# Transposing the memory's keys by crossbar DMA in a fused transformer block

## The chip, the cores and the metric

The kernel runs on one core of one Trainium2 chip. A core has TensorE (matrix products, into PSUM), VectorE, ScalarE and GpSimd (element-wise work), SyncE (here it only issues DMAs), 16 DMA engines, an on-chip memory of 128 partitions (SBUF) and eight PSUM banks of 128 x 512 f32. Each engine works through its own instructions in the order in which the program gives them, and waits on semaphores where it needs another engine's result. The metric is the device time of one execution in microseconds (us). In the profile PE is TensorE, PEld its weight load, DVE is VectorE, ACT ScalarE, POOL GpSimd, SP SyncE.

## What is computed

One layer on 256 tokens of width 1024, all in f32: a mixer (pooling over windows for half of the width, causal attention with 8 heads for the other half), cross attention to a memory of 256 rows with 4 heads of 256, and a convolutional feed-forward part. The change concerns the keys of the cross attention:

```python
def _cross_attention(h, m, w_xq, w_xkv, xq_norm_g, xk_norm_g, w_xo):
    q = (h @ w_xq).reshape(B, S, XATTN_HEADS, XATTN_HEAD_DIM)
    kv = (m @ w_xkv).reshape(B, M, 2, XATTN_HEADS, XATTN_HEAD_DIM)
    k, v = kv[:, :, 0], kv[:, :, 1]
    q = _rms_norm(q, xq_norm_g)
    k = _rms_norm(k, xk_norm_g)
    s = jnp.einsum('bshd,bmhd->bhsm', q, k) * (XATTN_HEAD_DIM ** -0.5)
    p = jax.nn.softmax(s, axis=-1)
    o = jnp.einsum('bhsm,bmhd->bshd', p, v).reshape(B, S, D_MODEL)
    return o @ w_xo
```

## The kernel before

**Products in two halves.** Each f32 operand is written as a high part (rounded to the type of TensorE's fast f32 products) and the low rest. `part_h` makes the high part on ScalarE (L269 without, L271 with a scale), `part_l` the rest on VectorE (L275, L277). Activations lie as 128 x 2048 tiles of such pairs (`cat`, `h`, `kx`, `xq` and so on; four buffers, called `pair`). The weights come from HBM in chunks of 1 MB into a ring of three (`raw`), loaded on SP's queue (L182). A chunk is two units; each unit is cast by ScalarE (`split_h`, L210, into `wh`) and its rest formed by VectorE (`split_l`, L221, into `wl`). `need(u)` issues these ahead of the unit u that TensorE uses, by up to five units, fewer at some stages. A load waits until the chunk three before it has been split.

**Stages.** TensorE runs: products of x for keys, queries, values and the pooled half; the memory's keys in two products of four units each (`a_chunk(18, ...)` for heads 0 and 1, `a_chunk(22, ...)` for heads 2 and 3); the mixer's output w_out (`resid_stage`, from u = 26, eight blocks f of 2.8 us, result `h`); w_xq (from u = 34, eight blocks, result `xq`, through L892 on ScalarE, L893 on VectorE, then `part_h`, a square and `part_l`); the memory's values; cross attention's output; the feed-forward part.

**Order by hand.** Whatever accompanies the products is written as generators ("jobs"). After every few matmuls the program calls `tick()`, and each job then issues its next piece; `wait(n)` lets n ticks go by. The constants WAIT_... are these numbers of ticks. A tick is two of the eight parts of a block in the stages w_out and w_xq, that is a quarter of a block. Within a tick the jobs take their turn in the order in which they were started: attention before the pool, the pool before the scores' later parts and before the key jobs. An engine's order is the order in which pieces were issued, so a piece that waits holds up all later ones of its engine. `finish` calls ticks until jobs have ended; between the memory's keys and w_out four ticks pass so, while the attention's last pieces are issued.

**The key job.** `key_job(c, bks)` takes the two PSUM banks of heads 2c and 2c+1 (each 128 memory rows x 512, two heads of 256). Five ticks after its start ScalarE sums the squares (L727), then `head_scale` makes 1/sqrt by Newton steps on GpSimd (`rs4y`, `rs5y`, L249 to L252). Eight ticks later VectorE scales the first bank into the SBUF tile `kn` (L735), seven ticks later the second. Nine ticks later TensorE transposes the first head in four 128 x 128 transposes (L743) into one bank, and ScalarE's `part_h` writes `kx`; thirteen ticks later `part_l`, two ticks later the second head in the same manner. The job ends 57 ticks after its start. `x_job(hp)` uses `kx` in the score products of w_xq's stage (in `three`, L286 to L288): the first, for heads 0 and 1, is issued eight ticks after w_xq's fourth block and once both key jobs have ended.

**The pool and the attention at the start of w_out.** The pool's result is evacuated in two steps of two groups (`evac_split` in `pool_job`: L271 and L277 per group, two groups to a bank), two ticks apart. Then the attention's four banks are evacuated (`evac_split` in `attn_job`, L269 and L275). All go into `cat`, w_out's input.

**Buffers.** PSUM banks are handed out by `bank()` from eight; small SBUF tiles of 128 x 512 f32 by `t2()` from nineteen.

## Time and profile before

| | |
|---|---|
| time of the kernel, median of 3 runs (least to most) | 380.37 us (379.93 to 380.6) |
| span of the profiled execution, first to last instruction | 378.1 us |
| median of the runs above that span | 2.27 us |
| instructions | 5948 |
| mean granted TensorE clock | 0.999 |
| moved from and to HBM | 67.71 MB read, 1.05 MB written |

The span is the profiled execution's own time as the profile gives it; what an execution takes before its first and after its last instruction is in the runs' times alone. The page gives the busy time of each engine, then the chain of work that ended last, then groups of instructions. A line of the timeline has the start (us from the span's start), the duration, the engine, the line of the kernel, the operation, the tiles written and read, and in brackets the engine's idle time before it with the instruction that ended it. Consecutive instructions of one kind are merged (x2, x4), so their duration is that of the whole run. Durations of pipelined instructions overlap: what one costs its engine is the distance from its start to the next one's.

### The profile page before, as it was taken

Reading aid. Unit: us, or ns where it says so; the run is one execution under the profiler, and the core shown is the slowest. Engines: PE = TensorE matmul, PEld = TensorE weight load, DVE = VectorE, ACT = ScalarE, POOL = GpSimd, SP = SyncE. Lnnn points to the kernel's source line nnn. Section 1 sums busy time; section 2 is a strip of 40 time slices with the busy share of each in tenths; the row PEclk is TensorE's granted clock in tenths of the full one; section 3 lists DMA queues with packets and bytes.
Section 4 is the critical chain, followed back from the end, with each engine's and each line's share of the span. In section 5 each row is a group of like instructions: output and inputs, shape, how many; then the busy total and the mean of one; then the engine's idle time right before and its main releaser. Section 6 shows DMA issues by size and latency. Waiting matters only on the chain.

```text
span 378.1 us, 5948 instructions
## 1 busy us (share of the span) xinstructions
PE 373.9 (99%) x2154; PEld 325.7 (86%) x2154; DVE 317.6 (84%) x572; ACT 248.2 (66%) x483; POOL 70.6 (19%) x151
## 2 busy tenths in 40 slices
PE   9999999999999999999999999999999999999996
PEld 7888888888888988898888888888888888888885
DVE  4699999979878969689979999999999999654461
ACT  5767986977567665855665588778877786633210
POOL 0253886043731142101220000000000000000000
PEclk9999999999999999999999999999999999999999
DMA  8995372454505636263635155665555645364500
GB/s 265 421 383 217 121 327 93 146 208 139 198 5 217 224 111 225 109 224 112 219 118 221 59 179 210 223 220 184 179 206 213 224 136 199 128 246 161 201 16 28
DMA packets 12412, 69.13 MB, mean 183 GB/s; under 512 B 1376, under 2 KB 2784, under 8 KB 4832
## 3 DMA queue, kind: packets, MB, share of 16 engines
q1 hardware_dynamic: 12096, 68.24, 50.1%
q10 hardware_dynamic: 288, 0.52, 0.4%
q8 instruction: 17, 0.28, 0.3%
q14 instruction: 11, 0.09, 0.1%
HBM read 67.71 MB, written 1.05 MB: 182 GB/s over the span
## 4 chain that ended last, share of the span: by engine, by line
PE 99%; DVE 0%; issue 0%
PE bank L301 42%; PE bank L300 22%; PE bank L414 8%; PE bank L419 8%; PE bank L416 8%; PE bank L1065 1%; PE bank L288 1%; PE bank L286 1%; PE bank L287 1%; PE bank L372 1%; PE bank L572 1%; PE bank L1067 1%; PE bank L611 1%; PE bank L883 0%; PE bank L743 0%; PE bank L494 0%
## 5 line engine op out<-in xcount | busy, mean ns | idle before, releaser
L221 DVE TENSOR_TENSOR wl<-raw,wh 128x1024 fp32r<-128x1024 f32 (+1 forms) x127 | 150.0, 1197 | 3.9 <-ACT wh L210 3.9
L210 ACT CAST wh<-raw 128x1024 fp32r<-128x1024 f32 (+1 forms) x125 | 126.0, 1028 | 35.1 <-DMA raw<-wpack 31.0
L301 PE MATMUL bank<-hs,wh 128*128 128x512 f32 x304 | 105.4, 391 | 0.0
L300 PE MATMUL bank<-hs,wl 128*128 128x256 f32 x304 | 85.2, 280 | 0.0
L301 PEld LDWEIGHTS bank<-hs,wh 128*128 128x128 f32 x304 | 56.9, 187 | 12.4
L300 PEld LDWEIGHTS bank<-hs,wl 128*128 128x128 f32 x304 | 57.5, 189 | 0.0
L301 PE MATMUL bank<-act,wh 128*128 128x512 f32 x154 | 53.4, 391 | 0.0
L300 PE MATMUL bank<-act,wl 128*128 128x256 f32 x154 | 43.2, 280 | 0.0
L998 ACT ACTIVATE y<-up,sc 128x256 f32<-128x256 f32 x44 | 26.2, 603 | 22.3 <-DVE up L985 17.7
L301 PE MATMUL bank<-h,wh 128*128 128x512 f32 x112 | 39.4, 394 | 0.0
L1005 DVE SCALAR_TENSOR_TENSOR y<-up,sc,y 128x255 f32<-128x255 f32 (+1 forms) x88 | 36.6, 476 | 0.0
L301 PEld LDWEIGHTS bank<-act,wh 128*128 128x128 f32 x154 | 28.8, 187 | 6.3
L300 PE MATMUL bank<-h,wl 128*128 128x256 f32 x112 | 31.7, 283 | 0.0
L300 PEld LDWEIGHTS bank<-act,wl 128*128 128x128 f32 x154 | 29.1, 189 | 0.0
L301 PEld LDWEIGHTS bank<-h,wh 128*128 128x128 f32 x112 | 21.0, 188 | 4.6
L1069 DVE TENSOR_TENSOR o<-bank,sc 128x256 f32<-128x256 f32 x8 | 3.4, 424 | 24.5 <-PE bank L301 21.4
L301 PE MATMUL bank<-cat,wh 128*128 128x512 f32 x62 | 21.8, 393 | 0.0
L301 PE MATMUL bank<-ox,wh 128*128 128x512 f32 x62 | 21.6, 394 | 0.0
L271 ACT ACTIVATE h<-sc 128x256 fp32r<-128x256 f32 x16 | 8.2, 510 | 20.3 <-DVE sc L789 20.2
L300 PEld LDWEIGHTS bank<-h,wl 128*128 128x128 f32 x112 | 21.2, 189 | 0.0
L414 PE MATMUL bank<-wh,mg 128*128 128x512 f32 x64 | 20.7, 405 | 0.0
L797 POOL TENSOR_TENSOR h_acc<-h_sq,h_acc 128x256 f32<-128x256 f32 x14 | 12.9, 921 | 41.6 <-ACT h_sq L796 41.5
(253 smaller groups left out, 712.2 us busy)
## 6 DMA issues: line engine op xcount, KB each, us to landing
raw<-wpack SPq DMA_DIRECT2D x59, 1024.0 KB, 4.8
raw<-wpack SPq DMA_DIRECT2D x4, 512.0 KB, 7.3
mraw<-memT SPq DMA_DIRECT2D x4, 256.0 KB, 8.3
out<-o SPq DMA_DIRECT2D x8, 128.0 KB, 1.9
sc<-xpack SPq DMA_DIRECT2D x3, 256.0 KB, 5.1
raw<-wpack ACTq DMA_DIRECT2D x2, 256.0 KB, 3.5
raw<-wpack SPq DMA_DIRECT2D x2, 256.0 KB, 4.6
tab<-table SPq DMA_DIRECT2D x1, 480.0 KB, 8.8
```

The source lines that it names most:

```text
L210: copy(split[u][0][:, r], unit(u)[:, r])
L221: dve.tensor_tensor(l[:, r], unit(u)[:, r], h[:, r].bitcast(F32), op=ALU.subtract)
L271: act.activation(h, src, AF.Copy, scale=scale)
L286: pe.matmul(o, stat[0], mov[0], start=start, stop=False)
L300: pe.matmul(b[:, 0:n], stat[1], mov[:, 0:n], start=start, stop=False, skip_group_check=not wide_first)
L301: pe.matmul(b, stat[0], mov, start=False, stop=stop, skip_group_check=not wide_first)
L414: pe.matmul(bk[tt], a[tt][0], wv[0], start=k == 0, stop=False)
L416: pe.matmul(bk[tt], a[tt][1], wv[0], start=False, stop=False)
L419: pe.matmul(bk[tt], a[tt][0], wv[1], start=False, stop=k == KT - 1)
L797: pool.tensor_tensor(acc, sq, acc, op=ALU.add)
L998: act.activation(y[:, g * S:(g + 1) * S], src[:, g * S:(g + 1) * S], AF.Identity, bias=col(sc, C_CB + f), scale=col(sc, C_CW + 2 * 2 * NFF ...
L1005: dve.scalar_tensor_tensor(yy[:, j:], uu[:, :S - j], col(sc, C_CW + (2 - j) * 2 * NFF + f), yy[:, j:], op0=ALU.mult, op1=ALU.add)
```

## The change

The sixteen transposes on TensorE and the four banks for them go. In their place, for each of the two key jobs: ScalarE splits each scaled tile `kn` (128 x 512 f32) into two planes of 16-bit halves, lower halves first, then upper ones (128 x 1024 half-words, tile `kp`); SP issues a crossbar-transposing DMA from `kp` to `kf` for each of the two tiles; ScalarE then joins the halves, two copies of 512 half-words for each head, into a tile `kT` that has the layout of the old PSUM bank. `part_h` and `part_l` read `kT` in SBUF. Two key jobs make four splits, four transposing DMAs and eight joins.

The pauses of the job change too. The first tile's split follows its scaling with no tick between for heads 0 and 1, after one tick for heads 2 and 3; the second tile is scaled six ticks after the first tile's split and split three ticks (one tick) later; the DMAs follow three (two) ticks later, the first join twenty (eighteen) ticks after them. Six tiles for each job are taken from the nineteen `t2` buffers.

```diff
-WAIT_KEY = [0, 8, 7, 2, 0, 13, 5]
+WAIT_KEY = [0, 8, 6, 0, 0, 0, 5]
+WAIT_FLAT = [[0, 3, 3, 20, 1, 4], [1, 1, 2, 18, 2, 4]]
...
         yield from wait(WAIT_KEY[1])
+        flat = []
         for mt in range(TT):
             for i in range(2):
                 r = slice(i * XD, (i + 1) * XD)
                 dve.tensor_scalar(kn[c, mt][:, r], bks[mt][:, r], col(y, 2 * mt + i), None, op0=ALU.mult)
-            yield from wait(WAIT_KEY[2])
+            yield from wait(WAIT_FLAT[c][mt])
+            planes = t2(f"kp{c}{mt}").bitcast(U16)
+            act.copy(planes.rearrange("p (z n) -> p z n", z=2),
+                     kn[c, mt].bitcast(U16).rearrange("p (n z) -> p z n", z=2))
+            flat.append((planes, t2(f"kf{c}{mt}").bitcast(U16)))
+            if mt == 0:
+                yield from wait(WAIT_KEY[2])
+        pauses = WAIT_FLAT[c]
+        yield from wait(pauses[2])
+        for planes, to in flat:
+            nc.sync.dma_start_transpose(to.rearrange("p (g s) -> p g s", g=8), planes)
+        yield from wait(pauses[3])
         for i in range(2):
             h = 2 * c + i
-            yield from wait(WAIT_KEY[3])
-            b = bank()
-            for dd in range(2):
-                for mt in range(TT):
-                    pe.transpose(b[:, (dd * 2 + mt) * P:(dd * 2 + mt + 1) * P],
-                                 kn[c, mt][:, i * XD + dd * P:i * XD + (dd + 1) * P], ident)
-            bb = b.rearrange("p (d s) -> p d s", d=2)
-            yield from wait(WAIT_KEY[4])
+            kT = t2(f"kT{c}{i}")
+            for mt in range(TT):
+                act.copy(kT.bitcast(U16).rearrange("p (d m s z) -> p m z d s", d=2, m=2, z=2)[:, mt],
+                         flat[mt][1].rearrange("p (z i d s) -> p i z d s", z=2, i=2, d=2)[:, i])
+                yield from wait(pauses[4])
+            bb = kT.rearrange("p (d s) -> p d s", d=2)
             part_h(kxv[0][:, 2 * h:2 * h + 2], bb)
-            yield from wait(WAIT_KEY[5])
+            yield from wait(pauses[5])
             part_l(kxv[1][:, 2 * h:2 * h + 2], bb, kxv[0][:, 2 * h:2 * h + 2])
```

More of the change, by code (lines that the diff above doesn't have):

```diff
@@ L12 @@
 I32 = mybir.dt.int32
+U16 = mybir.dt.uint16
 AF = mybir.ActivationFunctionType
```

## The prediction

> **What bounds the kernel now.** I read the page first, then the chain that ended last, then the matmuls around the work that the change takes off TensorE.
>
> ```profile
> PE 373.9 (99%) x2154; PEld 325.7 (86%) x2154; DVE 317.6 (84%) x572; ACT 248.2 (66%) x483; POOL 70.6 (19%) x151
> PE 99%; DVE 0%; issue 0%
> ```
>
> TensorE is busy 99% of the span and makes up 99% of the chain, at full granted clock. So any time that its queue is spared comes off the end, and any gap that opens in it is added. The other engines matter only where TensorE comes to wait for them. Here is what one group of key transposes (L743) costs:
>
> ```profile
> 102.56 0.39 PE L301 MATMUL bank<-cat,wh 128*128 128x512 f32 x1
> 102.79 0.28 PE L300 MATMUL bank<-cat,wl 128*128 128x256 f32 x1
> 102.91 0.39 PE L301 MATMUL bank<-cat,wh 128*128 128x512 f32 x1
> 103.14 0.60 PE L743 MATMUL bank<-tab,kn 128*128 128x128 f32 x4
> 103.50 0.36 PE L300 MATMUL bank<-cat,wl 128*128 128x256 f32 x1
> 103.70 0.40 PE L301 MATMUL bank<-cat,wh 128*128 128x512 f32 x1
> ```
>
> Columns: start, duration, engine, line. Durations overlap, so starts have to be compared. From one L301 to the next is 0.35 us without transposes (102.56 to 102.91), and 0.79 with four between (102.91 to 103.70). A group costs 0.44 us, not the 4 x 0.27 that its instructions last.
>
> **What it removes.** Four such groups:
>
> ```profile
> L743 PE MATMUL bank<-tab,kn x16: 270/272/273, 92.3 to 115.5; 128*128 128x128 f32 x16
> ```
>
> Sixteen transposes are four groups of four; at the same price each, 4 x 0.44 = 1.76 us leave TensorE. The PSUM banks that go with them are not scarce: no matmul in this stretch starts late for one.
>
> **What it adds to ScalarE.** Four copies that split a 128x512 f32 tile into planes (1024 half-words per partition each) and eight that join 512 half-words. Nearest rows by element count:
>
> ```profile
> L210 ACT CAST wh<-raw 128x1024 fp32r<-128x1024 f32 x14 | 14.3, 1038 | 0.0
> L206 ACT CAST misc<-raw 128x512 fp32r<-128x512 f32 x3 | 1.8, 618 | 2.8 <-DMA raw<-wpack 2.8
> L269 ACT CAST kx<-bank 128x512 fp32r<-128x512 f32 x4 | 2.2, 574 | 0.0
> 111.43 1.98 ACT L210 CAST wh<-raw 128x1024 fp32r<-128x1024 f32 x2
> ```
>
> 4 x 1.04 + 8 x 0.62 = 9.1 us. No row shows 16-bit or strided elements; half of this (twice the elements in a given time) or double are the bounds, and I take the rows. The casts into kx stay, from SBUF at 0.62 instead of 0.57. What counts is where these copies stand in ScalarE's queue.
>
> **First place: the start of the w_out stage.** The first split of heads 0 and 1 follows the scaling of `kn` (L735) with no tick between. It therefore precedes, in ScalarE's queue, the pool's second evacuation (L271/L277, groups 2 and 3), which is emitted two ticks later:
>
> ```profile
> 81.88 0.39 ACT L623 COPY pt<-bank 128x256 f32<-128x256 f32 x1
> 82.14 0.50 ACT L271 ACTIVATE cat<-bank,sc 128x256 fp32r<-128x256 f32 x1
> 82.75 0.88 DVE L735 TENSOR_SCALAR kn<-bank,rs4y 128x256 f32<-128x256 f32 x2 [0.50 <-POOL rs4y L252]
> 83.54 0.47 DVE L277 SCALAR_TENSOR_TENSOR cat<-bank,sc,cat 128x256 fp32r<-128x256 f32 x1
> 84.05 0.47 ACT L271 ACTIVATE cat<-bank,sc 128x256 fp32r<-128x256 f32 x1 [1.41 <-DVE cat L277]
> 84.56 0.48 DVE L277 SCALAR_TENSOR_TENSOR cat<-bank,sc,cat 128x256 fp32r<-128x256 f32 x1 [0.54 <-ACT cat L271]
> 85.90 0.50 PE L297 MATMUL bank<-cat,wh 128*128 128x512 f32 x1
> ```
>
> Today ScalarE does group 2 at 82.14, before `kn` is scaled. With the split in front, it waits for L735 (82.75 + 0.88 = 83.63), copies, and is free about 0.95 later, at 84.6 (two casts of 1.04 take 1.98 together, so one is followed 0.95 after its start). Then the chain runs as the rows show it: L277 starts 0.51 after L271 (84.05 to 84.56), and the next L271 starts when that L277 ends (83.54 + 0.47, then 84.05). Group 2: 84.61, L277 85.12 to 85.60; group 3: 85.64, L277 86.15 to 86.63. That end is at 85.04 today. The w_out stage's first matmul needs a bank; going by the order in which the code takes and frees the eight banks, its bank is the one that groups 2 and 3 leave. So it starts at 86.69 (0.06 behind) instead of 85.90: **+0.79 us**. The cover of today is 0.86 us (85.04 to 85.90), and the delay is 1.59.
>
> The profile itself names another release for that start:
>
> ```profile
> 85.90 0.19 PEld L297 LDWEIGHTS bank<-cat,wh 128*128 128x128 f32 x1 [0.17 <-DVE cat L275]
> 84.96 1.23 DVE L275 TENSOR_TENSOR cat<-bank,cat 128x256 fp32r<-128x256 f32 x3
> 86.76 0.87 DVE L735 TENSOR_SCALAR kn<-bank,rs4y 128x256 f32<-128x256 f32 x2
> ```
>
> That is the attention's evacuation, L275, which stands behind group 3's L277 on VectorE. In the change the second L735 moves one tick forward (6 for 7) and so ahead of the L275s: 86.55 + 0.8, so the first L275 ends near 87.8 and the stage would start 1.9 us late. Bounds 0 (if the copy slips in elsewhere) and 1.9; I take 0.79, because the first L275 ended at about 85.4, too early to be what 85.90 waited for.
>
> **Second place: the crossbar transfers.** Each pair of transposes (256 KB each) is issued on SP's queue behind the second split of its heads, and later read by ScalarE.
>
> ```profile
> 88.82 0.33 SPq L182 DMA_DIRECT2D raw<-wpack  x1
> 92.35 0.33 SPq L182 DMA_DIRECT2D raw<-wpack  x1
> 98.86 0.33 SPq L182 DMA_DIRECT2D raw<-wpack  x1
> 112.41 3.48 SPq L182 DMA_DIRECT2D raw<-wpack  x2
> raw<-wpack SPq DMA_DIRECT2D x59, 1024.0 KB, 4.8
> raw<-wpack ACTq DMA_DIRECT2D x2, 256.0 KB, 3.5
> out<-o SPq DMA_DIRECT2D x8, 128.0 KB, 1.9
> q10 hardware_dynamic: 288, 0.52, 0.4%
> ```
>
> A tick is two blocks of 0.35, 0.70 us. Counted in ticks, the first join of heads 0 and 1 comes 16 ticks after the old first transposes (92.3), at about 104.2 on the changed clock (0.79 later); that of heads 2 and 3 comes 12 after 104.28, at about 112.5 (0.88 taken off, 0.79 added). ScalarE ends the second splits near 92 and 103. The transposes queue behind the loads issued at 88.82 and 98.86, which land at 93.6 and 103.7, half a microsecond to one later when delayed with the rest. So a pair may take some 9.7 and 8.4 us before ScalarE waits. Behind SP's wait for the splits stand the next loads: the one of 92.35, whose data ScalarE first casts at 111.43 (it lands near 97, so some 14 us of cover), and that of 112.41, which comes long after the issue at 103. Nothing is lost there.
>
> The trace has no crossbar transfer. Bounds for one of 256 KB: 1.9 us (the store of half the size) to 5.4 us: its 1024 runs of 128 half-words, if each costs what one packet of the ACT queue costs (0.4% of 16 x 378.1 us by 288 packets, 84 ns), spread over 16 engines. I take 3.5, the load of the same bytes; the pair 7, or less where the two overlap. That lands in time, with about 1.4 us to spare on the second pair.
>
> The Trainium skill is of two minds here. "VectorE: DVE Perf Modes", section "The three transpose paths", gives 1309 ns for one 128x128 block by the DMA crossbar against 390 ns by TensorE; by that figure, with the 16 blocks of a pair in series, a pair would be estimated at 21 us, ScalarE would stand still twice, and the sum would pass 400 us. "Advanced Engine Details and Errata", section "X-Bar Transpose (TRN2)", has such transfers as fast as ordinary ones, 350 to 400 GB/s, by which a pair would be estimated at 1.5 us and cost nothing. No row before can decide.
>
> **Third place: the w_xq stage.** ScalarE's load there:
>
> ```profile
> 104.00:109.40 5.40, 5.40 (x35) 4.78 (x34) 3.60 (x9) 3.41 (x8) 1.49 (x2) 1.00 0.00 0
> 109.40:115.00 5.60, 5.60 (x35) 4.95 (x34) 5.09 (x9) 3.58 (x7) 2.02 (x2) 1.00 0.24 67
> 115.00:121.00 6.00, 6.00 (x38) 5.28 (x37) 4.76 (x8) 4.57 (x12) 1.21 (x3) 1.00 0.75 287
> 121.00:127.00 6.00, 6.00 (x36) 5.20 (x35) 5.36 (x8) 4.90 (x11) 0.79 (x1) 1.00 0.50 178
> 107.31 1.05 ACT L269 CAST kx<-bank 128x512 fp32r<-128x512 f32 x2
> 122.78 0.36 ACT L892 COPY xq<-bank 128x256 f32<-128x256 f32 x1
> 124.65 0.96 DVE L277 SCALAR_TENSOR_TENSOR xq<-xq,ggx,xq 128x256 fp32r<-128x256 f32 x1
> 127.10 0.28 PE L286 MATMUL bank<-kx,xq 128*128 128x256 f32 x1
> 128.41 0.29 PE L288 MATMUL bank<-kx,xq 128*128 128x256 f32 x1
> ```
>
> The fourth figure after the span is ScalarE: 13.05 of 17.6 us from 109.4 to 127. Five of the eight joins (3.1 us) and two kx casts that run at 107.3 today fall there: 17.3 of 17.6. The evacuation of xq block 3 (L892 at 122.78) slips by about 3 us. Its low half is done at 125.6 today, and the score product that starts at 127.10 needs it as its twelfth matmul, at 128.41, which the change brings forward by about 1: 127.5. So 2.8 us of cover become nearly 2, against a slip of 3 less what VectorE gains by meeting one kx subtraction (0.68) later. Bounds 0 and 1; I take **+0.1**. The casts of weights have more room. The end of the key work in ticks stays where it is (57 after the job's start in both).
>
> **The sum**, against the profiled span: 378.1 - 1.76 + 0.79 + 0.1 = 377.2 us. The three runs have a median of 380.37, 2.27 above that span. So **379.5 us**, 0.2% less.
>
> **The rivals.**
> - *The whole gain*: the split costs TensorE nothing, because L735 or the copy runs earlier or shorter than I have it. For it: a copy of half the price, and L735 0.5 us earlier (it waits for POOL), take away 1.0 of the 1.59 and bring the start to 85.9. Against it: four instructions in a fixed order. 378.1 - 1.76 + 2.27 = 378.6.
> - *The attention's bank*: the stage waits for L275 as the profile names it. 378.1 - 1.76 + 1.9 + 0.1 + 2.27 = 380.6, no change.
> - *Late transposes* (the other side): from 8.4 us per pair on, ScalarE stops at a join with its queue behind it: the evacuations of w_out blocks 6 and 7, the weight casts. At 10.8 us, my upper row bound, the first pair is 1.1 and the second 2.4 us late; ScalarE has no room after the second, so TensorE pays about 2.4: 381.9, slower by 0.4%. Each further microsecond per pair adds up to two. The Trainium skill's 1309 ns, cited above, is this case at its worst. For late transposes speak pieces of 256 bytes, when the weight loads move longer ones; against them, the DMA rows are empty from 104 to 109.4 (share 0.00), where most of the second pair falls.
>
> **How the numbers follow.** Forecast 0.50, whole gain 0.17, attention's bank 0.13, late transposes 0.20. A measurement of this kernel can tell about 0.2% (0.76 us) from no change, so faster means under 379.6. The forecast with its bounds lies across that line, 0.27 and 0.23: faster 0.27 + 0.17 = 0.44, same 0.23 + 0.13 = 0.36, slower 0.20. The range takes the whole gain in at the bottom (378.4) and late transposes up to the row bound at the top (381.9).
>
> **What would show it.** No L743 on TensorE; L297 at about 86.7 with a gap before it (at 85.9 or 87.8 the first or second rival holds); one L271 at 84.6 behind a 1.04 us copy; transposes that land within 8 us of the load ahead; joins that start without a wait for DMA; the score product's start at about 126.2 with no gap inside it. A join that waits for DMA, or splits far from 1.04 us, would prove me wrong.

## The result and the profile after

| | before | after |
|---|---|---|
| time, median (least to most, runs) | 380.34 us (379.93 to 380.6, 4) | 385.12 us (384.81 to 385.48, 4) |
| ratio of the times, 95% interval | | 1.0126 (1.0112 to 1.014) |
| span of the profiled execution | 378.1 us | 382.9 us |

The forecast was 379.5 us in a range of 378.4 to 381.9. The kernel is 4.8 us slower, 3.2 us beyond the range.

From the page of the changed kernel, the busy times, the DMA packets and the engines' shares in the chain that ended last:

```profile
PE 374.1 (98%) x2138; PEld 323.8 (85%) x2138; DVE 317.2 (83%) x572; ACT 257.3 (67%) x495; POOL 69.8 (18%) x151
DMA packets 16636, 70.18 MB, mean 183 GB/s; under 512 B 5600, under 2 KB 7008, under 8 KB 9056
PE 73%; DVE 9%; ACT 9%; POOL 4%; issue 3%; DVEq 0%; POOLq 0%
```

The chain was 99% TensorE; now a quarter of it runs through other engines. TensorE waits for them at these places (view of the waits, TensorE's alone, from 83 to 170 us: matmul, whom it waited for, us in total, times, longest):

```profile
PE bank L895 <- DVE xp L885: 1.8, 3, 0.8
PE bank L302 <- ACT h L273: 1.2, 1, 1.2
PE bank L299 <- DVE cat L279: 0.7, 1, 0.7
PE bank L302 <- DVE wl L223: 0.5, 1, 0.5
PE bank L290 <- DVE xq L279: 0.2, 1, 0.2
```

The changed kernel's line numbers are two higher in the helpers: L299, L302 and L303 are the matmuls called L297, L300 and L301 before, L273 and L279 the high and low part with a scale, L801 the addition (L789) that starts a block of h, L885 and L895 the normalised scores and their transposes (L873 and L883).

**Where the time went.** I matched TensorE's matmuls of the two traces by their tiles and order and subtracted their starts, with the difference at 84.5 us set to zero. The heads are times in the trace of before; the last column is also the shift at the end.

| shift, us, at | 90 | 105 | 113 | 116 | 127 | 140 | 150 | 170 |
|---|---|---|---|---|---|---|---|---|
| changed kernel | +0.78 | -0.56 | +1.30 | +0.86 | +1.38 | +1.87 | +3.72 | +4.92 |

The w_out stage starts 0.78 late; three groups of transposes give 1.34 back by 105; 1.86 are lost at once near 112; the fourth group gives 0.44 back; then the w_xq stage and the two score jobs lose 4.06. From 170 us on nothing changes.

Timeline of TensorE in the changed kernel, with the gaps' beginnings and ends:

```profile
86.60 0.50 PE L299 MATMUL bank<-cat,wh 128*128 128x512 f32 x1 [0.70 <-DVE cat L279]
...
111.14 0.39 PE L303 MATMUL bank<-h,wh 128*128 128x512 f32 x1
112.73 0.38 PE L302 MATMUL bank<-h,wl 128*128 128x256 f32 x1 [1.20 <-ACT h L273]
113.25 0.49 PE L303 MATMUL bank<-h,wh 128*128 128x512 f32 x1
...
144.78 0.55 PE L895 MATMUL bank<-tab,xp 128*128 128x128 f32 x3 [0.71 <-DVE xp L885]
...
161.56 0.55 PE L895 MATMUL bank<-tab,xp 128*128 128x128 f32 x3 [0.77 <-DVE xp L885]
```

The matmuls at 112.73 and 113.25 are the first that use block 7 of h, the last one. What made it late is in the timelines of ScalarE and VectorE of the changed kernel:

```profile
107.03 0.51 ACT L273 ACTIVATE h<-sc 128x256 fp32r<-128x256 f32 x1 [1.04 <-DVE sc L801]
...
107.76 1.40 ACT L755 COPY kT<-kf 128x512 uint16<-128x512 uint16 x2
109.19 0.62 ACT L271 CAST kx<-kT 128x512 fp32r<-128x512 f32 x1
109.71 0.51 ACT L273 ACTIVATE h<-sc 128x256 fp32r<-128x256 f32 x1
...
112.17 0.51 ACT L273 ACTIVATE h<-sc 128x256 fp32r<-128x256 f32 x1 [0.97 <-DVE sc L801]
```

```profile
110.25 0.49 DVE L279 SCALAR_TENSOR_TENSOR h<-sc,h 128x256 fp32r<-128x256 f32 x1 [1.40 <-ACT h L273]
110.66 0.68 DVE L277 TENSOR_TENSOR kx<-kT,kx 128x512 fp32r<-128x512 f32 x1
111.26 0.88 DVE L801 TENSOR_TENSOR sc<-bank,sc 128x256 f32<-128x256 f32 x2
```

And the same block in the kernel before (rows of VectorE and of TensorE):

```profile
109.79 0.88 DVE L789 TENSOR_TENSOR sc<-bank,sc 128x256 f32<-128x256 f32 x2 [0.32 <-PE bank L301]
111.25 0.48 DVE L277 SCALAR_TENSOR_TENSOR h<-sc,h 128x256 fp32r<-128x256 f32 x1
112.02 0.28 PE L300 MATMUL bank<-h,wl 128*128 128x256 f32 x1
112.14 0.39 PE L301 MATMUL bank<-h,wh 128*128 128x512 f32 x1
```

Two joins and a cast stand in ScalarE's queue ahead of block 6's high part, which therefore starts at 109.71 (behind two casts, at 108.45, before). VectorE, whose queue is in order too, waits 1.40 for it with the addition of block 7 (L801) behind. The rows of before show what I had not looked at. The low part of block 7 ended at 111.25 + 0.48 = 111.73, and the matmul that needs it, the counterpart of the one at 113.25, started at 112.14, 0.41 later. In run 5 below such a matmul starts 0.06 after the low part, so 0.35 us were to spare. VectorE had stood idle 0.32 for TensorE ahead of block 7's addition. Together that is about 0.7 us, all the room that there was for a delay of VectorE, or for a TensorE that comes early.

### The profile page after: what moved, and what is told of

Its sections match the earlier page's. It is cut to its first block, busy times and chain, and to the rows that moved or that the text cites. A ratio compares the mean times of both kernels' runs of the same rounds, so it can differ in the third digit from the quotient of the medians.

```text
span 382.9 us, 5940 instructions
## 1 busy us (share of the span) xinstructions
PE 374.1 (98%) x2138; PEld 323.8 (85%) x2138; DVE 317.2 (83%) x572; ACT 257.3 (67%) x495; POOL 69.8 (18%) x151
## 2 busy tenths in 40 slices
DMA packets 16636, 70.18 MB, mean 183 GB/s; under 512 B 5600, under 2 KB 7008, under 8 KB 9056
## 4 chain that ended last, share of the span: by engine, by line
PE 73%; DVE 9%; ACT 9%; POOL 4%; issue 3%; DVEq 0%; POOLq 0%
PE bank L303 34%; PE bank L302 18%; PE bank L416 5%; PE bank L418 5%; PE bank L421 5%; DVE wl L223 3%; ACT wh L212 2%; PE bank L1077 1%; ACT kT L755 1%; ACT xp L877 1%; ACT p L603 1%; PE bank L374 1%; DVE sc L801 1%; DVE kn L738 1%; PE bank L574 1%
## 5 line engine op out<-in xcount | busy, mean ns | idle before, releaser
L303 PE MATMUL bank<-hs,wh 128*128 128x512 f32 x304 | 105.4, 391 | 0.0
L302 PE MATMUL bank<-hs,wl 128*128 128x256 f32 x304 | 85.1, 280 | 0.0
L303 PEld LDWEIGHTS bank<-hs,wh 128*128 128x128 f32 x304 | 56.8, 187 | 12.5
L302 PEld LDWEIGHTS bank<-hs,wl 128*128 128x128 f32 x304 | 57.5, 189 | 0.0
L303 PE MATMUL bank<-act,wh 128*128 128x512 f32 x154 | 53.4, 391 | 0.0
L302 PE MATMUL bank<-act,wl 128*128 128x256 f32 x154 | 43.1, 280 | 0.0
L303 PE MATMUL bank<-h,wh 128*128 128x512 f32 x112 | 39.4, 393 | 0.1
L303 PEld LDWEIGHTS bank<-act,wh 128*128 128x128 f32 x154 | 28.8, 187 | 6.3
L302 PE MATMUL bank<-h,wl 128*128 128x256 f32 x112 | 31.8, 284 | 1.7 <-ACT h L273 1.2
L302 PEld LDWEIGHTS bank<-act,wl 128*128 128x128 f32 x154 | 29.1, 189 | 0.0
L303 PEld LDWEIGHTS bank<-h,wh 128*128 128x128 f32 x112 | 21.0, 187 | 4.8 <-DVE h L279 0.3
L302 PEld LDWEIGHTS bank<-h,wl 128*128 128x128 f32 x112 | 21.1, 189 | 2.3 <-ACT h L273 1.5
L303 PE MATMUL bank<-cat,wh 128*128 128x512 f32 x62 | 21.6, 394 | 0.0
L303 PE MATMUL bank<-ox,wh 128*128 128x512 f32 x62 | 21.6, 394 | 0.0
L416 PE MATMUL bank<-wh,xg 128*128 128x512 f32 x64 | 20.6, 404 | 0.0
```

Source lines behind the costliest of these rows:

```text
L302: pe.matmul(b[:, 0:n], stat[1], mov[:, 0:n], start=start, stop=False, skip_group_check=not wide_first)
L303: pe.matmul(b, stat[0], mov, start=False, stop=stop, skip_group_check=not wide_first)
L416: pe.matmul(bk[tt], a[tt][0], wv[0], start=k == 0, stop=False)
```

## The experiments

At first there were three theories: A, the joins hold up ScalarE's queue; B, VectorE is behind from the start of w_out on; C, the crossbar DMAs or their issue disturb the weight loads.

**1. Joins left out** (keys not transposed).

```diff
-            kT = t2(f"kT{c}{i}")
+            kT = kn[c, i]
             for mt in range(TT):
-                act.copy(kT.bitcast(U16).rearrange("p (d m s z) -> p m z d s", d=2, m=2, z=2)[:, mt],
-                         flat[mt][1].rearrange("p (z i d s) -> p i z d s", z=2, i=2, d=2)[:, i])
                 yield from wait(pauses[4])
```

> Leaves out the eight joins: kx is made from kn, untransposed, so the keys are wrong; splits, transposing DMAs and all pauses stay. Theory A (the joins, standing in ScalarE's queue ahead of the evacuations of w_out and w_xq, are what opened the gaps after 110 us): only the gap at the start of w_out (0.8 us) stays against the 1.75 us saved, so about 379.4 us. Theory B (VectorE, set back 1.4 us at the start of w_out, carries its lag to the end of that stage): part of the gaps stays, about 382 us. Theory C (the crossbar DMAs and SP's longer issues disturb the weight loads): still 384 to 385 us.

Measured: 380.96 us, ratio to before 1.0013 (1.0003 to 1.0022). 4.2 of the 4.8 us are the joins'. But the rest lies between A and B: although all four groups of transposes are gone, the kernel is no faster than before.

**2. The first split later.** The first split of heads 0 and 1, and the second scaling with it, go behind the attention's evacuation.

```diff
-WAIT_FLAT = [[0, 3, 3, 20, 1, 4], [1, 1, 2, 18, 2, 4]]
+WAIT_FLAT = [[8, 2, 2, 20, 1, 4], [1, 1, 2, 18, 2, 4]]
...
-                yield from wait(WAIT_KEY[2])
+                yield from wait(WAIT_KEY[2] if c else 0)
```

> The first split of heads 0 and 1 and the scaling of their second tile move behind the attention's evacuation (first split 8 ticks after its scaling in place of 0; all later pieces at their old ticks or one later). The gap at the start of w_out should go under every theory. Theory A: nothing else moves, 385.1 less 0.8, about 384.3 us. Theory B: VectorE loses no time there, so the gaps at 112 us and behind it go as well for the most part, about 381 us. Theory C: 384.3 us.

Measured: 384.74 us, ratio 1.0116 (1.0101 to 1.0131). The gap at the start of w_out goes entirely (shift 0.00 at 90 us, -1.34 at 105), but of the 0.78 that this brings the gap near 112 takes 0.47 back: +0.99 at 113, +4.58 at the end, against +4.92. So TensorE's earlier start there was worth 0.34 of 0.78: w_out does not end when TensorE is through but when the last block of h is there. B, which expected 381 us, falls; A and C expected 384.3.

**3 and 4. The DMAs alone, and the change without them.** First, the kernel before issues four crossbar transposes of `kn` that nobody reads. Then, the changed kernel without its DMAs, with joins that read the planes themselves (keys not transposed).

```diff
+        for mt in range(TT):
+            to = t2(f"kf{c}{mt}").bitcast(U16)
+            nc.sync.dma_start_transpose(to.rearrange("p (g s) -> p g s", g=8), kn[c, mt].bitcast(U16))
```

```diff
-        for planes, to in flat:
-            nc.sync.dma_start_transpose(to.rearrange("p (g s) -> p g s", g=8), planes)
...
-                         flat[mt][1].rearrange("p (z i d s) -> p i z d s", z=2, i=2, d=2)[:, i])
+                         flat[mt][0].rearrange("p (z i d s) -> p i z d s", z=2, i=2, d=2)[:, i])
```

> The kernel before, with four crossbar-transposing DMAs of the same size issued on SP at the ticks of the changed kernel, from kn into tiles that nothing reads. Theories A and B: 380.3 us, no change. Theory C: 383 us or more.

> The changed kernel without its four transposing DMAs: the joins read the planes as they are, so the keys are not transposed. ScalarE's work is the same. Theories A and B: as the changed kernel, 385.1 us. Theory C: 382 us or less.

Measured: 380.41 us, ratio 1.0006 (0.9995 to 1.0016), and 385.15 us, ratio 1.0126 (1.0111 to 1.0141). Added, the DMAs cost nothing; taken away, they bring nothing. C falls.

**5. Before, without the transposes.** The other parts of the change are not there: this is what TensorE's saving is worth by itself.

```diff
-            b = bank()
-            for dd in range(2):
-                for mt in range(TT):
-                    pe.transpose(b[:, (dd * 2 + mt) * P:(dd * 2 + mt + 1) * P],
-                                 kn[c, mt][:, i * XD + dd * P:i * XD + (dd + 1) * P], ident)
-            bb = b.rearrange("p (d s) -> p d s", d=2)
+            bb = kn[c, i].rearrange("p (d s) -> p d s", d=2)
```

> The kernel before with its sixteen transposes of the keys left out: the keys are read from kn as they stand, so the keys are not transposed; nothing else is added. Theory 1, the prediction's premise (whatever TensorE's queue is spared comes off the end): 4 x 0.44 = 1.76 us less, 378.6 us. Theory 2 (the last block of h, made by ScalarE and VectorE, sets the end of w_out in absolute time, since its low part ends at 111.73 and TensorE takes it at 111.79; only the group after it can count): the three groups before 112 us are handed back in a gap ahead of the last block of h, 0.4 us less at most, 379.9 to 380.4 us. A result near 379.2 would give half to each.

Measured: 379.92 us, ratio 0.999 (0.9981 to 1.0): 0.4 of 1.76 us. The first rows are TensorE's, the next VectorE's, of this run:

```profile
110.63 0.39 PE L301 MATMUL bank<-h,wh 128*128 128x512 f32 x1
111.08 0.38 PE L300 MATMUL bank<-h,wl 128*128 128x256 f32 x1
111.60 0.50 PE L301 MATMUL bank<-h,wh 128*128 128x512 f32 x1
```

```profile
111.06 0.48 DVE L277 SCALAR_TENSOR_TENSOR h<-sc,h 128x256 fp32r<-128x256 f32 x1
```

TensorE is 1.34 ahead at 105 us. Its matmuls stand 0.35 for two apart in this stage; here 0.45 and 0.52 pass between one and the next, and the second of them waits for block 7's low part, ready at 111.06 + 0.48 = 111.54. 0.71 is handed back here; the 0.63 that pass are near the 0.67 of room (0.32 and 0.35) counted above. The fourth group makes it 1.03, and another 0.53 is handed back at the scores' transposes at 157 us, which wait for xp (rows of VectorE and TensorE):

```profile
156.06 0.62 DVE L868 TENSOR_SCALAR xp<-xp,xrec 128x256 f32<-128x256 f32 x2
156.47 0.55 PE L878 MATMUL bank<-tab,xp 128*128 128x128 f32 x3 [0.32 <-DVE xp L868]
```

Theory 1 falls, and the number is theory 2's. The mechanism of theory 2 holds only in part: the matmul at 111.79 on which it rests uses block 6 of h (block 7 is used from 112.02 on), so about half of the first three groups' gain gets past w_out, and what the end keeps is settled at the scores.

**6. Joins on GpSimd.**

```diff
-                act.copy(kT.bitcast(U16).rearrange("p (d m s z) -> p m z d s", d=2, m=2, z=2)[:, mt],
+                pool.tensor_copy(kT.bitcast(U16).rearrange("p (d m s z) -> p m z d s", d=2, m=2, z=2)[:, mt],
```

> The changed kernel with its eight joins on GpSimd instead of ScalarE, in the same places; splits, crossbar DMAs and results unchanged. Theory 1 (the loss is the joins' time in ScalarE's queue): near the run without joins, 381 us, with at most 0.5 us more if GpSimd makes the last sums of h's squares late. Theory 2 (the loss lies in the later kx casts and in the keys coming later, whoever joins them): 384 to 385 us. Theory 3 (GpSimd takes more than 2 us for one join, so the keys come late to the scores): above 385 us, with the score products waiting for kx.

Measured: 384.36 us, ratio 1.0107 (1.0092 to 1.0122). By its number this is theory 2, but the trace gives another reason, ScalarE's row:

```profile
110.73 0.62 ACT L271 CAST kx<-kT 128x512 fp32r<-128x512 f32 x1 [2.29 <-POOL kT L755]
```

The cast follows the joins too closely: ScalarE stands 2.29 us at it, with block 6 of h behind. The run moved the wait and decided nothing; runs 11 to 15 mend it.

**7. Joins of heads 0 and 1 only** (heads 2 and 3 not transposed).

```diff
-            kT = t2(f"kT{c}{i}")
+            kT = t2(f"kT{c}{i}") if c == 0 else kn[c, i]
             for mt in range(TT):
-                act.copy(kT.bitcast(U16).rearrange("p (d m s z) -> p m z d s", d=2, m=2, z=2)[:, mt],
-                         flat[mt][1].rearrange("p (z i d s) -> p i z d s", z=2, i=2, d=2)[:, i])
+                if c == 0:
+                    act.copy(kT.bitcast(U16).rearrange("p (d m s z) -> p m z d s", d=2, m=2, z=2)[:, mt],
+                             flat[mt][1].rearrange("p (z i d s) -> p i z d s", z=2, i=2, d=2)[:, i])
```

> The changed kernel with the four joins of heads 2 and 3 left out (kx of these heads is read from kn, not transposed), the four of heads 0 and 1 in place. Theory 1 (each pair of joins is paid where it stands): the gap ahead of h's last block stays as in the changed kernel (+1.76 us in two steps near 112 us), the later steps at 125 and 130 us go, the scores' transposes give back most of the rest: 381.5 to 383 us. Theory 2 (the lateness of ScalarE that the first pair starts is never made good, since the w_xq stage has no room): 384 to 385 us. If the second pair alone does the harm: 381 us.

Measured: 382.84 us, ratio 1.0066 (1.0051 to 1.0081). Each pair of heads is paid where it stands: +1.33 at 113 us as in the changed kernel, but +0.75 at 140 where that has +1.87.

**8. The first joins spread**, one piece per block of h.

```diff
-WAIT_FLAT = [[0, 3, 3, 20, 1, 4], [1, 1, 2, 18, 2, 4]]
+WAIT_FLAT = [[0, 3, 3, 15, 4, 4], [1, 1, 2, 18, 2, 4]]
```

> The changed kernel with the first pair's joins moved: the first comes 15 ticks behind the DMAs for 20, then one piece each four ticks, one per block of h, so that no two stand together ahead of a block of h. The same work. Theory 1 (place: two joins and a cast together ahead of the block before the last, 1.26 us, make h's last block late): the gap near 112 us shrinks from 1.76 to 0.6 us as without joins; what follows at 125 us and later stays: 383.5 to 384.3 us, or less if the saved time carries through. Theory 2 (amount: any join in this stretch costs its 0.77 us of ScalarE): no change from 385.1 us.

Measured: 384.71 us, ratio 1.0114 (1.0097 to 1.0131). The gap near 112 shrinks as theory 1 has it (shift -0.06 at 113 us), and 1.9 us open at the next place (TensorE):

```profile
124.12 0.40 PE L303 MATMUL bank<-h,wh 128*128 128x512 f32 x1
126.22 0.36 PE L302 MATMUL bank<-h,wl 128*128 128x256 f32 x1 [1.70 <-DVE wl L223]
```

These are the weights of w_xq's block 5. ScalarE casts them at 122.06 (119.32 before), behind three joins, one of which has moved there, and VectorE forms their low part behind a kx subtraction (0.68) that has moved there too. In this run, as in run 2, time won at one place is for the most part lost at the next: of the 1.36 us won near 112 us 0.49 are left at the end.

**9 and 10. VectorE's backlog.** The scaling of heads 2 and 3 goes from VectorE to ScalarE, once without the transposes and once in the kernel before.

```diff
+                if c:
+                    act.activation(kn[c, mt][:, r], bks[mt][:, r], AF.Copy, scale=col(y, 2 * mt + i))
+                else:
                     dve.tensor_scalar(kn[c, mt][:, r], bks[mt][:, r], col(y, 2 * mt + i), None, op0=ALU.mult)
```

> The kernel before with the sixteen transposes left out (keys read from kn, not transposed), and with the scaling of heads 2 and 3 (four instructions, 1.7 us of VectorE at 95.6 and 99.9 us) on ScalarE instead of VectorE. Theory 1 (VectorE's backlog between 90 and 104 us makes h's last block late, and with it gone TensorE's saving counts): the gap of 0.6 us near 112 us goes, 378.6 to 379.3 us. Theory 2 (a limit other than VectorE's queue holds the last block of h, or the saving is lost further on): 379.9 us as without this move.

> The kernel before, with only the scaling of heads 2 and 3 on ScalarE instead of VectorE. Theory 1: before, TensorE alone is on the path (no gap near 112 us to close), so no change: 380.2 to 380.5 us. Theory 2 (VectorE costs the kernel time there already): 379.5 us or less.

Measured: 379.06 us, ratio 0.9961 (0.9942 to 0.9981), and 380.47 us, ratio 1.0 (0.9991 to 1.001). VectorE in run 9:

```profile
108.73 0.88 DVE L787 TENSOR_TENSOR sc<-bank,sc 128x256 f32<-128x256 f32 x2 [0.83 <-PE bank L301]
```

Now VectorE waits 0.83 for TensorE before block 7 (0.32 before), and the shift is -1.80 at 116 us, all four groups, and -1.51 at the end. The same move is worth nothing as long as TensorE has the transposes. The two queues bound the stretch together: sparing one alone gains 0.4 or 0.0, both 1.3 us (0.44, 0.00 and 1.51 by the shifts).

**11 and 12. The crossbar way off ScalarE.** The splits of heads 0 and 1 and all joins go to GpSimd, a pair's joins ahead of both its casts; the casts and subtractions of heads 0 and 1 come behind the last block of h. Run 12 adds the scaling of run 9.

```diff
-WAIT_FLAT = [[0, 3, 3, 20, 1, 4], [1, 1, 2, 18, 2, 4]]
+WAIT_FLAT = [[0, 3, 3, 13, 1, 2, 1, 13, 2, 2, 2], [1, 1, 2, 16, 1, 1, 1, 4, 3, 0, 4]]
-            act.copy(planes.rearrange("p (z n) -> p z n", z=2),
-                     kn[c, mt].bitcast(U16).rearrange("p (n z) -> p z n", z=2))
+            (act.copy if c else pool.tensor_copy)(
+                planes.rearrange("p (z n) -> p z n", z=2),
+                kn[c, mt].bitcast(U16).rearrange("p (n z) -> p z n", z=2))
...
+        kTs = [t2(f"kT{c}{i}") for i in range(2)]
         for i in range(2):
...
             for mt in range(TT):
...
+                yield from wait(pauses[3 + 2 * i + mt])
+                pool.tensor_copy(kTs[i].bitcast(U16).rearrange("p (d m s z) -> p m z d s", d=2, m=2, z=2)[:, mt],
+                                 flat[mt][1].rearrange("p (z i d s) -> p i z d s", z=2, i=2, d=2)[:, i])
+        for i in range(2):
+            h = 2 * c + i
+            bb = kTs[i].rearrange("p (d s) -> p d s", d=2)
+            yield from wait(pauses[7 + 2 * i])
             part_h(kxv[0][:, 2 * h:2 * h + 2], bb)
-            yield from wait(pauses[5])
+            yield from wait(pauses[8 + 2 * i])
             part_l(kxv[1][:, 2 * h:2 * h + 2], bb, kxv[0][:, 2 * h:2 * h + 2])
```

> The changed kernel with the two splits of heads 0 and 1 and all eight joins on GpSimd, the joins of a pair ahead of both its casts, and the casts of heads 0 and 1 behind the last block of h. Theory 1 (the loss is ScalarE's: its queue ahead of the last block of h and in the w_xq stage; the crossbar way itself costs nothing): near the run of before without transposes, 379.9 to 380.6 us. Theory 2 (GpSimd's copies slow VectorE down, or the keys come late): 382 us or more.

> The run before this one (splits of heads 0 and 1 and all joins on GpSimd, late casts), and the scaling of heads 2 and 3 on ScalarE. Theory 1 (with ScalarE's queue and VectorE's backlog both out of the way, the 1.76 us that TensorE is spared come off the end): 378.7 to 379.5 us, faster than both kernels. Theory 2 (only ScalarE's queue was in the way): 379.9 to 380.6 us, as without this move.

Measured: 381.42 us, ratio 1.0027 (1.0017 to 1.0036), and 381.08 us, ratio 1.0019 (1.001 to 1.0029). Neither theory has the number. In run 12 the whole 1.80 us are there at 116 and 127 us, so theory 1 is right that far; they and 0.9 more are handed back by 170, at the scores. These start with a reduction on VectorE, behind VectorE's work on w_xq's blocks; its row before, and in runs 9 and 12:

```profile
130.56 0.68 DVE L851 TENSOR_REDUCE ssx<-bank 128x4 f32<-128x512 f32 x1
```

```profile
129.56 0.68 DVE L849 TENSOR_REDUCE ssx<-bank 128x4 f32<-128x512 f32 x1
```

```profile
131.84 0.68 DVE L868 TENSOR_REDUCE ssx<-bank 128x4 f32<-128x512 f32 x1
```

In the changed kernel:

```profile
135.52 0.68 DVE L863 TENSOR_REDUCE ssx<-bank 128x4 f32<-128x512 f32 x1
```

TensorE is 1.8 us early in run 12, and the reduction 1.0 late (1.28, less the 0.26 by which this run's trace is behind at 84.5 us). For why, the groups by shape between 110 and 128 us, before and in run 12:

```profile
L221 DVE TENSOR_TENSOR wl<-raw,wh 128x1024 fp32r<-128x1024 f32 x6 | 7.6, 1265 | 0.2 <-ACT wh L210 0.2
...
L275 DVE TENSOR_TENSOR kx<-bank,kx 128x512 fp32r<-128x512 f32 x3 | 2.0, 680 | 0.0
...
L221 DVE TENSOR_TENSOR wl<-raw,wh 128x512 fp32r<-128x512 f32 x2 | 1.4, 684 | 0.0
```

```profile
L277 DVE TENSOR_TENSOR kx<-kT,kx 128x512 fp32r<-128x512 f32 x4 | 4.3, 1084 | 0.0
...
L223 DVE TENSOR_TENSOR wl<-raw,wh 128x512 fp32r<-128x512 f32 x2 | 2.1, 1068 | 0.0
```

```profile
L758 POOL COPY kT<-kf 128x512 uint16<-128x512 uint16 x8 | 8.5, 1125 | 0.0
```

(The last row is GpSimd's, from 103 to 128 us.) VectorE has one more kx subtraction there, and its instructions of 512 elements take half as long again on average. Both could be the cause.

**13 to 15.** Three edits of run 12: without the joins (keys not transposed); the four kx subtractions on GpSimd; the joins of heads 0 and 1 on ScalarE again, one per block of h, with casts a few ticks earlier.

```diff
-        kTs = [t2(f"kT{c}{i}") for i in range(2)]
+        kTs = [kn[c, i] for i in range(2)]
...
-                pool.tensor_copy(kTs[i].bitcast(U16).rearrange("p (d m s z) -> p m z d s", d=2, m=2, z=2)[:, mt],
-                                 flat[mt][1].rearrange("p (z i d s) -> p i z d s", z=2, i=2, d=2)[:, i])
```

```diff
-            part_l(kxv[1][:, 2 * h:2 * h + 2], bb, kxv[0][:, 2 * h:2 * h + 2])
+            pool.tensor_tensor(kxv[1][:, 2 * h:2 * h + 2], bb, kxv[0][:, 2 * h:2 * h + 2].bitcast(F32),
+                               op=ALU.subtract)
```

```diff
-WAIT_FLAT = [[0, 3, 3, 13, 1, 2, 1, 13, 2, 2, 2], [1, 1, 2, 16, 1, 1, 1, 4, 3, 0, 4]]
+WAIT_FLAT = [[0, 3, 3, 13, 4, 4, 4, 0, 4, 2, 4], [1, 1, 2, 16, 1, 1, 1, 4, 3, 0, 4]]
...
-                pool.tensor_copy(kTs[i].bitcast(U16).rearrange("p (d m s z) -> p m z d s", d=2, m=2, z=2)[:, mt],
+                (pool.tensor_copy if c else act.copy)(
+                    kTs[i].bitcast(U16).rearrange("p (d m s z) -> p m z d s", d=2, m=2, z=2)[:, mt],
```

> The kernel with splits of heads 0 and 1 on GpSimd and scaling of heads 2 and 3 on ScalarE, with the eight joins on GpSimd left out: kx is read from kn, not transposed; the DMAs run and are read by nobody. Theory 1 (the joins on GpSimd slow VectorE's instructions beside them, wl of 512 elements from 0.68 to 1.4 us, and make the score chain late): the waits at 128 and 141 us go, 379.2 to 379.9 us. Theory 2 (the two kx subtractions moved into the w_xq stage, 1.4 us of VectorE, do it): 380.7 to 381.1 us, as with the joins.

> The kernel with splits of heads 0 and 1 and all joins on GpSimd and scaling of heads 2 and 3 on ScalarE, with the four kx subtractions on GpSimd too. Theory 1 (VectorE's queue in the w_xq stage makes the score chain late, and 4 x 0.68 us taken from it lets the saving through): 379.2 to 380.2 us, faster than before or level with it. Theory 2 (GpSimd's work slows VectorE as much as it takes from it, or GpSimd's longer subtraction makes the keys late): 381 us or more.

> The kernel with splits of heads 0 and 1 on GpSimd, joins of heads 2 and 3 on GpSimd and scaling of heads 2 and 3 on ScalarE; the joins of heads 0 and 1 go back to ScalarE, one in each block of h from the fifth on, where it stands idle for 1.2 to 1.7 us, and their kx casts and subtractions come a few ticks earlier. Theory 1 (GpSimd's joins slow VectorE): half of that slowing goes, 380.2 to 380.8 us. Theory 2 (any further copy in ScalarE's queue ahead of the last blocks of h costs): 382 us or more.

Measured: 379.92 us, ratio 0.9982 (0.9967 to 0.9996); 380.86 us, ratio 1.0003 (0.9993 to 1.0014); 381.12 us, ratio 1.0011 (1.0001 to 1.0022). The joins on GpSimd cost 1.2 us (run 12 against run 13; 1.03 by the shifts, +0.90 and -0.13 at the end). VectorE does the same instructions in both runs, so one can be laid beside the other; a kx subtraction in run 12, while GpSimd copies, and the same one in run 13:

```profile
115.17 1.20 DVE L277 TENSOR_TENSOR kx<-kT,kx 128x512 fp32r<-128x512 f32 x1
```

```profile
114.40 0.68 DVE L277 TENSOR_TENSOR kx<-kn,kx 128x512 fp32r<-128x512 f32 x1
```

Such stretched instructions put VectorE 1.0 us behind by the scores' reduction. Not all of the averages above is the copies' doing: two of the four kx subtractions take 1.2 us in run 13 too, beside GpSimd's sums of squares. Run 14 takes four subtractions from VectorE and gains 0.2 (0.30 by the shifts; the times alone do not tell the two runs apart); its groups on VectorE (110 to 128 us) and GpSimd (103 to 128 us):

```profile
L223 DVE TENSOR_TENSOR wl<-raw,wh 128x1024 fp32r<-128x1024 f32 x6 | 9.6, 1600 | 0.0
```

```profile
L766 POOL TENSOR_TENSOR kx<-kT,kx 128x512 fp32r<-128x512 f32 x4 | 7.2, 1820 | 0.1
```

The subtraction takes 1.82 us on GpSimd, and VectorE's weights take 1.60 on average (1.33 in run 12, 1.27 before) and the low parts of xq 1.23 (0.59 in run 12): 4.2 us for the 4.3 that VectorE was spared. Run 14 lies between its theories, nearer the second. Run 15 also lies between its theories and is no better than run 12. Run 14 is the best of the complete crossbar versions, level with before; none was found that beats it.

**16 and 17. Only the places.** Run 1 and run 13 without splits and DMAs, which leaves run 5 and run 9 with the kx casts and subtractions at the places of run 1 and run 13. The edit to run 1 (that to run 13 takes away the same):

```diff
-            planes = t2(f"kp{c}{mt}").bitcast(U16)
-            act.copy(planes.rearrange("p (z n) -> p z n", z=2),
-                     kn[c, mt].bitcast(U16).rearrange("p (n z) -> p z n", z=2))
-            flat.append((planes, t2(f"kf{c}{mt}").bitcast(U16)))
...
-        for planes, to in flat:
-            nc.sync.dma_start_transpose(to.rearrange("p (g s) -> p g s", g=8), planes)
```

> The kernel before with the sixteen transposes left out and the pauses of the changed kernel: the kx casts and subtractions stand at the changed kernel's places, without splits, crossbar DMAs and joins (keys read from kn, not transposed). Theory 1 (the splits cost the 1.0 us between 379.92 and 380.96 us): 379.8 to 380.1 us. Theory 2 (the later casts and subtractions cost it): 380.8 to 381.1 us.

> The kernel before with the sixteen transposes left out, scaling of heads 2 and 3 on ScalarE, and the casts and subtractions of all heads late, in the w_xq stage; without splits, crossbar DMAs and joins (keys read from kn, not transposed). Theory 1 (the splits cost the 0.9 us between 379.06 and 379.92 us): 379.0 to 379.3 us. Theory 2 (the two casts and subtractions of heads 0 and 1 in the w_xq stage cost it): 379.7 to 380.1 us.

Measured: 379.99 us, ratio 0.9991 (0.9982 to 1.0001), so in the changed kernel's places the splits make the 1.0 us between runs 5 and 1; and 380.11 us, ratio 0.9995 (0.9986 to 1.0005), so run 13's 0.9 us over run 9 (1.38 by the shifts) are its late casts and subtractions. Run 17 has run 13's shifts at every column: the splits (two on GpSimd, two on ScalarE) and the DMAs that run 13 has besides cost nothing there. What run 12 hands back, from -1.80 to +0.90, is thus 0.29 that run 9 loses too, 1.38 for the late casts and subtractions and 1.03 for the joins on GpSimd.

**The account.** The shifts of the runs that build the change up part by part:

| shift, us, at | 90 | 105 | 113 | 116 | 127 | 140 | 150 | 170 | time, us |
|---|---|---|---|---|---|---|---|---|---|
| 5: transposes out | 0.00 | -1.34 | -0.63 | -1.03 | -1.03 | -0.98 | -0.97 | -0.44 | 379.92 |
| 16: and later kx casts | 0.00 | -1.34 | -0.76 | -1.17 | -1.17 | -1.17 | -1.17 | -0.33 | 379.99 |
| 1: and splits, DMAs | +0.77 | -0.32 | +0.48 | +0.07 | +0.07 | +0.07 | +0.07 | +0.87 | 380.96 |
| 7: and joins of heads 0, 1 | +0.76 | -0.58 | +1.33 | +0.92 | +0.72 | +0.75 | +1.22 | +2.41 | 382.84 |
| changed kernel | +0.78 | -0.56 | +1.30 | +0.86 | +1.38 | +1.87 | +3.72 | +4.92 | 385.12 |

By the last shift: -0.44 for the transposes, +0.11 for the places, +1.20 for the splits, +1.54 for the first four joins, +2.51 for the other four; the sum is +4.92. Each figure is what a part costs on top of those in the rows above it; runs 2 and 8 show that a part is worth less where others stand in the way.

## Why the prediction was wrong

**"Any time that its queue is spared comes off the end."** This is the first step that failed. The group's price was right: the four take 1.80 off the shift in run 9. But run 5 shows that 0.44 of the 1.76 us reach the end. 99% busy says that nothing TensorE waits for is late; it doesn't say by how much it is early. Around block 7 of h there were 0.67 us of room. At the scores that the second job transposes there was almost none: before, the part of xp that the second of these transposes needs was ready at 156.28 + 0.35 = 156.63 and used at 156.75, in run 5 at 156.06 + 0.35 = 156.41 and at 156.47. Only because xp itself came about 0.4 earlier could 0.44 of run 5's 0.97 get through. With that, the rival "the whole gain" falls too. This alone makes no slower kernel; it takes the gain out of the forecast.

**First place, the start of w_out.** Right in mechanism and size: L299 starts at 86.60 where 86.69 was foretold, +0.78 for +0.79, and the split is what does it: run 16, which has the scaling at its new place but no split, starts w_out on time (shift 0.00 at 90 us), as does run 11 with the split on GpSimd. The rival "attention's bank" (87.8) is out. What the step did not see is that this delay, too, is worth less at the end (0.34 in run 2) than at its place.

**Second place, the crossbar transfers.** Right that nothing waits for them (runs 3 and 4). View of the tile `kf` in the changed kernel (durations in ns, then start times), SyncE's queue, and the landing of the last transfer alone:

```profile
L755 ACT COPY kT<-kf x8: 757/768/779, 107.8 to 126.6; 128x512 uint16<-128x512 uint16 x8
L749 SPq DMA_TRANSPOSE kf<-kp x4: 1237/1480/3748, 93.8 to 103.8; - x4
DMA to landing us min/median/max: 5.0/6.8/7.7
```

```profile
93.75 5.19 SPq L749 DMA_TRANSPOSE kf<-kp  x2
100.32 5.12 SPq L749 DMA_TRANSPOSE kf<-kp  x2
```

```profile
DMA to landing us min/median/max: 5.0/5.0/5.0
```

The first pair is issued from 93.75 on and has landed by 101.8; the last one from 100.32 on, its second transfer at 103.81, when the second split is done, and it has landed by 108.8: 8.0 and 8.5 us. The prediction counted from the landing of the loads that it gave as issued at 88.82 and 98.86 (here landed at 94.5 and 105.7); so counted they are 7.2 and 3.1 us, for the 7 taken and the 9.7 and 8.4 allowed. The step was right, with more cover than it claimed, since the first joins came at 107.76 and 118.45, not at 104.2 and 112.5. So a pair took neither the 21 us that the sentence from the Trainium skill, "VectorE: DVE Perf Modes", "The three transpose paths", was estimated to give, nor the 1.5 us from "Advanced Engine Details and Errata", "X-Bar Transpose (TRN2)". The rival "late transposes" got the sign right, but its mechanism is refuted: run 4 has no crossbar transfers and takes as long.

**The copies' prices.** Joins 0.77 us for 0.62 (row L755 above), 1.2 us more for the eight; the splits' row, from the view of the tile `kp`, is as foretold:

```profile
L741 ACT COPY kp<-kn x4: 1039/1046/1107, 83.6 to 102.7; 128x1024 uint16<-128x1024 uint16 x4
```

The splits cost 1.20 us at the end, on top of runs without joins; the forecast had 0.79 of it, as the first place.

**Third place, the w_xq stage: +0.1, at most 1.** This is the step that made the sign wrong. The joins cost 1.54 + 2.51 = 4.05 us. I weighed ScalarE's load (17.3 of 17.6 us) and then followed one consumer, the low part of xq block 3. The evacuation ahead of it slips by 4.45 us, not by 3 (ScalarE's row for 122.78 before):

```profile
127.23 0.35 ACT L904 COPY xq<-bank 128x256 f32<-128x256 f32 x1
```

Its score product waits only 0.2, because TensorE is late by then itself. Four things were missed. The joins were dated by TensorE's ticks, at 104.2 and 112.5. But a tick settles only where a piece stands in its engine's queue: TensorE ended block 5 of w_out at 103.56, VectorE came to its addition at 106.12 and ScalarE to its high part at 107.03, and the first join stands behind that. The first three joins were said to fall ahead of the stage and were followed no further; they stand ahead of blocks 6 and 7 of h, with 0.67 us of room. "The casts of weights have more room" was not worked out; TensorE waits 0.5 for weights, 1.7 in run 8. And a queue that is full stays late: ScalarE and VectorE pass the delay on to the reduction that starts the scores, 135.52 for 130.56, and TensorE pays it at L895 in both score jobs, the largest wait of all. The bounds "0 and 1" came from that one consumer; a stage with 0.3 us to spare and 0.15 more for each join had to have the whole added time in its upper bound.

In the terms of the sum, -1.76 + 0.79 + 0.1 = -0.87 was forecast for the span; the runs give -0.44 for the transposes, +0.11 for the places, +1.20 for the splits and +4.05 for the joins, +4.92 in all.

## What to carry to other kernels

That an engine is busy 99% of the time does not tell what sparing it gains: before counting a saving, look up how early each of its later operands is ready, and how far the engine that makes the operand could come forward itself; the place where the two together are smallest is the ceiling. Work moved to an engine with idle time has to be followed through that engine's queue to every later consumer, not to the nearest; where the sum of the load is nearly the length of the stage, the added time itself is the upper bound of the cost. Spreading the joins on the same engine moved the wait (run 8), and giving them and two splits to GpSimd, with the casts far enough behind, won back 3.7 of the 4.8 us (run 11). But a time clearly below that of the kernel before came only in runs that leave out the transposing itself, the lowest where two engines were spared at once (run 9).

## What the runs showed of the hardware

- A crossbar transpose of 128 x 1024 half-words holds SyncE's queue 1.24 to 3.75 us at its issue, where a plain load of 1 MB takes 0.33, and lands 5.0 to 7.7 us after the issue; the four added 4224 packets, all under 512 bytes (16636 for 12412, 5600 for 1376). Other loads were not delayed enough to show in the time (run 3).
- ScalarE's copy that interleaves half-words into its output takes 0.77 us for 512 of them, its copy of 512 f32 values 0.62; the split, which reads interleaved and writes in one run, takes the 1.04 us of 1024 f32 values.
- A VectorE subtraction of 128 x 512 with both operands in SBUF takes 1.20 us beside GpSimd's copies (run 12, at 115.17) and 0.68 without them (run 13, at 114.40); beside GpSimd's sums of squares two take 1.23 us in both runs. The Trainium skill, "SBUF — State Buffer", "Who interferes with whom", says that a VectorE instruction with two SBUF inputs contends with a GpSimd instruction that reads SBUF; the trace agrees with 0.68 against 1.20.
